# The last matrix product of a two-block transformer in fp32: 24 of its 32 row tiles by seven block products instead of eight, in two parts

## The chip, the core and the metric

One Trainium2 chip, one core. The time is device microseconds (us) of one launch of the whole kernel. An engine named PE is the matrix unit (TensorE), PEld its weight loads, DVE the vector engine, ACT the scalar engine, POOL the GpSimd engine, SP the sync engine, which here only starts transfers.

## What is computed

The input is x of 512 rows by 1024 columns, everything in fp32. Block one has two layers, each an attention and a SwiGLU network with layer norms; block two is one layer of a gated mixer and a network with a squared ReLU. Only the end of block two matters here:

```python
f = rmsnorm(h, pre_ff_g[l]) @ w_ff1[l]            # (512 x 1024) @ (1024 x 4096)
f = jnp.square(jax.nn.relu(f)) @ w_ff2[l]         # (512 x 4096) @ (4096 x 1024)
h = h + rmsnorm(f, post_ff_g[l])
```

The change concerns the product with `w_ff2`, called f2 below.

## The kernel before

**Precision.** Every fp32 operand v is split into hi (v rounded to the matrix unit's fp32r type) and lo = v - hi, and each product is three passes, hi*hi, hi*lo and lo*hi, accumulated in PSUM. For weights, ACT writes hi (line 125) and DVE subtracts to get lo (line 128); both land in a pair of 128 x 1024 tiles.

**Weights.** The class `Weights` streams all weights of the kernel in one list. A *spec* is one load of up to 512 KB into a raw tile (SP queue, line 79); a *unit* is what is split into one hi/lo pair. There are three raw buffers (`wraw`, line 244) and five pairs (line 245). When the matmuls of a unit are issued, `done` (line 157) frees it and `fill` (line 147) issues the splits of the unit five places ahead and the loads for which a raw buffer is free. SP takes its transfers strictly in the order written; a load waits there until the earlier readers of its buffer are through.

**Products by seven.** Some of the earlier products (`FAST`, `FAST1`, line 45) already go by Winograd's seven block products: two 2 x 2 block matrices are multiplied with seven products of blocks instead of eight, at the price of sums of blocks before and after. There the blocks of the weights are made on DVE (lines 100 to 107), the results are joined by the class `Blocks` (line 461). For these a raw buffer can be lent from another pool (`lent`, `lender`, lines 68 and 1308). `in_tiles` (line 429) runs the product with `w_ff1` (f1); its results, after ReLU and square, stand transposed in the tiles `h2` and `h3` (lines 1287 to 1317): 32 tiles of 128 x 512, tile k holding rows k of the inner 4096 for all 512 tokens.

**The last product, f2.** `Out` (line 364) and `out_phase` (line 387), called on line 1349. For each of the 32 row tiles k of `w_ff2`: load 512 KB, split it (ACT and DVE), split `h` tile k (lines 769 and 770, into `sh` and `sl`), then for each of four token tiles t three passes over two column halves, 24 matmuls of 128 x 128 by 128 x 512 on line 381. All eight PSUM banks are in use: four token tiles by two halves. The first 28 row tiles go k by k over all four t; the last four go t by t, so that the closing norm of one t (`finish_ff`, line 1322, and `last_tile`, line 1326) runs beside the matmuls of the next. This tail is not changed.

Order on the engines: the instructions are put in order by a scheduler from the program's order and their dependencies; SP alone keeps the written order (line 249).

Of the kernel before, what the change touches and what calls it, by code (L numbers as in the profile page):

```python
# [10 lines left out]
F32 = mybir.dt.float32  # L11
# [32 lines left out]

FAST, FAST1 = range(4, 22), range(4, 14)
# [9 lines left out]
class Weights:  # L55


    def __init__(self, nc, raw, pairs, specs, units, lent, n_raw, n_pairs):
        self.nc, self.raw, self.pairs, self.specs, self.units, self.lent = nc, raw, pairs, specs, units, lent
        self.room, self.n_pairs, self.lender = [n_raw, 1], n_pairs, None  # L60
        self.loaded, self.split, self.released = 0, 0, 0
        self.r, self.p, self.extra = {}, {}, set()

    def load(self, parts=0):
        i = self.loaded
        src, (a, b), n = self.specs[i]

        t = self.lender() if i in self.lent else self.raw.tile([128, 1024], F32, name="wraw")
        v = t[:, :a * b].rearrange("p (a b) -> p a b", a=a)
        if n is not None:  # L70
            self.nc.gpsimd.memset(t[:, :a * b], 0.0)
            v = v[:, :, :n]
        self.r[i] = t
        self.loaded += 1
        self.room[i in self.lent] -= 1
        if parts:
            part = lambda a, m: a[:, m * a.shape[1] // parts:(m + 1) * a.shape[1] // parts]
            return lambda m: self.nc.sync.dma_start(part(v, m), part(src, m))
        self.nc.sync.dma_start(v, src)

    def _used(self, i):
        self.room[i in self.lent] += 1
        return self.r.pop(i)

    def _source(self, i, part):
# [4 lines left out]
        while self.loaded <= i + (part not in (None, 0)):  # L90
            self.load()
        if part is None:
            return self._used(i)[:, :], None
# [7 lines left out]
        tt = self.nc.vector.tensor_tensor  # L101
# [9 lines left out]
    def _split(self, pool, steps=1, name=None):  # L111
# [10 lines left out]
        def step(steps):  # L122
            for s in steps:
                sl = slice(s * n, (s + 1) * n)
                self.nc.scalar.activation(hi[:, sl], t[:, sl], AF.Copy)  # L125
                if between:
                    between()
                self.nc.vector.tensor_tensor(lo[:, sl], t[:, sl], hi[:, sl].bitcast(F32), op=OP.subtract)  # L128
# [7 lines left out]
    def _loads(self):  # L136
        while self.loaded < len(self.specs) and self.room[self.loaded in self.lent]:
            self.load()
# [27 lines left out]
def body(ctx, tc, ins, out, stop=None, dbg=None):  # L166
# [11 lines left out]
    specs, units, lent, at = [], [], set(), {}  # L178

    def spec(key, w, r0, nk, c0, n, pad=None, unit=True):  # L180
# [3 lines left out]
        specs.append((cols(w, r0, nk, c0, n), (nk, pad or n), n if pad else None))  # L184

    def spec_pair(key, w, c0, c1, fast):
# [5 lines left out]
        for m, c in ((1, c1), (0, c0)) if fast else ((0, c0), (1, c1)):  # L192
            if fast and key[-1] >= 7 and len(specs) % 4 == 0:
                lent.add(len(specs))
# [45 lines left out]
    rows("f2", ins["w_ff2_2"], 32)  # L240
# [16 lines left out]
    W = Weights(nc, raw, pairs, specs, units, lent, 3, 5)  # L257

# [105 lines left out]
    class Out:  # L364


        def __init__(self, key, order, operand):
            self.key, self.order, self.operand = key, list(order), operand
            self.banks, self.act = {}, {}

        def __call__(self, k, t, halves=(0, 1)):
# [7 lines left out]
            for n, (a, b) in enumerate(((0, 0), (0, 1), (1, 0))):  # L379
                for c in halves:  # L380
                    nc.tensor.matmul(self.banks[t][c], act[a][:, ts(t)], w[b][:, 0, c * 512:(c + 1) * 512],  # L381
                                     start=first and n == 0, stop=last and n == 2)
# [4 lines left out]
    def out_phase(o, finish, after, tail, spare=None, last=None):  # L387
# [3 lines left out]
        head = o.order[:-tail]  # L391
# [6 lines left out]
        for t in range(NT):  # L398
# [8 lines left out]
            finish(t, o.banks[t])  # L407

# [372 lines left out]
    def ffn(l, tails, finish, after):  # L781
        with tc.tile_pool(name="h", bufs=6) as hp:
            four = [hp.tile([128, 4 * S], F32, name="h4") for _ in range(6)]
            h = [t[:, n * S:n * S + S] for t in four for n in range(4)]
            with tc.tile_pool(name="blocks", bufs=1) as bp:
# [5 lines left out]
                W.lender = lambda: room  # L791
# [511 lines left out]
    with tc.tile_pool(name="blocks2", bufs=1) as bp:  # L1303
# [9 lines left out]
        W.lender = lender  # L1313
# [3 lines left out]
    parts[1] = es3.enter_context(tc.tile_pool(name="h3", bufs=1)).tile([128, 4, S], F32, name="h3")  # L1317
    in_tiles(f1(14, 16), lambda n, p: evac_f1(n + 28, p))
    hs = es3.enter_context(tc.tile_pool(name="hs2", bufs=5))
# [6 lines left out]
    def last_tile(o, ks):  # L1326
# [47 lines left out]
```

## Time and profile before

| what | us |
|---|---|
| median of three runs (1737.64 to 1738.59) | 1737.68 |
| the profiled execution, own time | 1737.9 |
| its span, first to last instruction | 1736.2 |
| PE busy in the span | 1716.8 (99%) |
| DVE busy | 1202.5 (69%) |
| ACT busy | 858.2 (49%) |
| granted clock of PE over the span | 0.999 of full speed |

The profile is of one execution. Busy is the sum of an engine's instructions over the span of 1736.2 us. Matmuls overlap one another, so a busy share of PE near 100% says that it always had work, not how fast one matmul follows another; for that a run of matmuls is divided by its count. The time of the execution is 1.7 us more than its span.

### The profile page before, as it was taken

The numbers are of one execution on the slowest core, as the hardware profiler recorded it, in microseconds if no ns is written. First come the engines' busy times: TensorE is split into PE (matmuls) and PEld (weight loads), VectorE is DVE, ScalarE is ACT, GpSimd is POOL, SyncE is SP. The second block draws the span as 40 slices with busy tenths as digits, with TensorE's granted clock in tenths as the row PEclk, the third lists the DMA queues.
The fourth block names the chain that finished last, engine by engine and source line by source line (L and its number), as shares of the span: only waits on it lengthen the run. The fifth ranks groups of instructions, "written<-read, shape, count | busy, mean of one in ns | idle before, by whom it ended". The sixth has DMA issues, their size and how long they took to land.

```text
span 1736.2 us, 27322 instructions
## 1 busy us (share of the span) xinstructions
PE 1716.8 (99%) x10748; PEld 1531.6 (88%) x10748; DVE 1202.5 (69%) x2034; ACT 858.2 (49%) x1437; POOL 128.6 (7%) x237
## 2 busy tenths in 40 slices
PE   8999999999999999999999999999999999999998
PEld 8888889999978888888899999888877899988886
DVE  6888866999944656666789998346646588953333
ACT  6877633444533367777444445333525345652221
POOL 0312102000000012220000000001001100000000
PEclk9999999999999999999999999999999999999999
DMA  6544345434344245552333334331422223343331
GB/s 205 136 100 110 98 141 165 132 99 122 109 136 121 76 118 129 133 137 77 97 98 108 112 100 156 109 99 50 125 69 89 82 80 110 110 134 97 98 97 50
DMA packets 207202, 191.60 MB, mean 110 GB/s; under 512 B 8800, under 2 KB 176928, under 8 KB 207072
## 3 DMA queue, kind: packets, MB, share of 16 engines
q1 hardware_dynamic: 194384, 162.48, 31.8%
q0 software_dynamic: 12112, 25.52, 6.6%
q8 instruction: 85, 1.39, 0.3%
q10 hardware_dynamic: 576, 1.84, 0.3%
q14 instruction: 45, 0.37, 0.1%
HBM read 172.99 MB, written 7.38 MB: 104 GB/s over the span
## 4 chain that ended last, share of the span: by engine, by line
PE 91%; DVE 4%; ACT 3%; issue 1%; DMA 1%; POOL 0%; ACTq 0%; SPq 0%; POOLq 0%; DVEq 0%
PE ps L295 54%; PE ps L381 30%; PE ps L908 1%; PE ps L896 1%; PE ps L311 1%; PE ps L589 1%; PE ps L590 1%; DVE wlo L128 1%; ACT whi L125 1%; ACT x L634 1%; PE ps L695 0%; PE ps L719 0%; PE ps L1108 0%; PE ps L1113 0%; DMA x<-in_x 0%
## 5 line engine op out<-in xcount | busy, mean ns | idle before, releaser
L125 ACT ACTIVATE whi<-wraw 128x1024 fp32r<-128x1024 f32 (+2 forms) x332 | 332.9, 1010 | 290.8 <-PE ps L295 146.5
L128 DVE TENSOR_TENSOR wlo<-wraw,whi 128x1024 fp32r<-128x1024 f32 (+2 forms) x332 | 385.0, 1163 | 124.5 <-ACT whi L125 121.6
L295 PE MATMUL ps<-xh,whi 128*128 128x256 f32 (+1 forms) x1232 | 387.1, 316 | 1.0 <-ACT xh L313 1.0
L295 PE MATMUL ps<-xl,whi 128*128 128x256 f32 (+1 forms) x1232 | 385.4, 313 | 0.5 <-DVE xl L314 0.3
L295 PE MATMUL ps<-xh,wlo 128*128 128x256 f32 (+1 forms) x1232 | 385.6, 313 | 0.0
L295 PEld LDWEIGHTS ps<-xh,whi 128*128 128x128 f32 x1232 | 233.6, 190 | 14.4 <-ACT xh L313 2.4
L295 PEld LDWEIGHTS ps<-xh,wlo 128*128 128x128 f32 x1232 | 234.5, 190 | 12.9
L295 PEld LDWEIGHTS ps<-xl,whi 128*128 128x128 f32 x1232 | 234.6, 190 | 12.4 <-DVE xl L314 1.0
L295 PE MATMUL ps<-th,whi 128*128 128x256 f32 x736 | 204.2, 277 | 0.0
L295 PE MATMUL ps<-tl,whi 128*128 128x256 f32 x736 | 203.8, 277 | 0.0
L295 PE MATMUL ps<-th,wlo 128*128 128x256 f32 x736 | 203.5, 276 | 0.0
L295 PEld LDWEIGHTS ps<-tl,whi 128*128 128x128 f32 x736 | 138.5, 188 | 0.1
L295 PEld LDWEIGHTS ps<-th,whi 128*128 128x128 f32 x736 | 138.5, 188 | 0.1
L295 PEld LDWEIGHTS ps<-th,wlo 128*128 128x128 f32 x736 | 138.3, 188 | 0.0
L295 PE MATMUL ps<-whi,xh 128*128 128x256 f32 (+1 forms) x384 | 124.5, 324 | 0.0
L295 PE MATMUL ps<-whi,xl 128*128 128x256 f32 (+1 forms) x384 | 122.6, 319 | 0.0
L295 PE MATMUL ps<-wlo,xh 128*128 128x256 f32 (+1 forms) x384 | 122.5, 319 | 0.0
L381 PE MATMUL ps<-whi,th 128*128 128x512 f32 x312 | 96.8, 391 | 1.3 <-DVE h L523 1.1
L381 PE MATMUL ps<-whi,tl 128*128 128x512 f32 x312 | 96.1, 389 | 0.0
L381 PE MATMUL ps<-wlo,th 128*128 128x512 f32 x312 | 96.1, 389 | 0.0
L290 POOL TENSOR_TENSOR ln_st<-rs_in,mhalf 128x1 f32<-128x1 f32 x39 | 27.5, 704 | 824.6 <-DVE rs_in L289 817.6
L770 DVE TENSOR_TENSOR tl<-h,th 128x512 fp32r<-128x512 f32 x44 | 29.8, 690 | 79.1 <-ACT th L769 79.0
(347 smaller groups left out, 3139.2 us busy)
## 6 DMA issues: line engine op xcount, KB each, us to landing
wraw<-in_ffn_w_in SPq DMA_DIRECT2D x73, 512.0 KB, 4.8
wraw<-in_w_ff SPq DMA_DIRECT2D x60, 512.0 KB, 4.1
wraw<-in_ffn_w_out SPq DMA_DIRECT2D x44, 512.0 KB, 3.7
wraw<-in_a_w_qkv SPq DMA_DIRECT2D x23, 512.0 KB, 5.1
wraw<-in_w_in SPq DMA_DIRECT2D x20, 512.0 KB, 3.7
wraw<-in_kv_w SPq DMA_DIRECT2D x16, 512.0 KB, 3.9
room<-in_ffn_w_in SPq DMA_DIRECT2D x15, 512.0 KB, 3.9
copies<-extd POOLq DMA_DIRECT2D x16, 320.0 KB, 8.5
```

Source lines behind the costliest of these rows:

```text
L125: self.nc.scalar.activation(hi[:, sl], t[:, sl], AF.Copy)
L128: self.nc.vector.tensor_tensor(lo[:, sl], t[:, sl], hi[:, sl].bitcast(F32), op=OP.subtract)
L290: nc.gpsimd.tensor_tensor(r, u[:, :n], mhalf[:, :n], op=OP.pow)
L295: nc.tensor.matmul(ps, lhs[a][lsel], rhs[b][rsel], start=first and n == 0, stop=last and n == 2)
L311: nc.tensor.transpose(p[:, k, :], y[:, ts(4 * c + k)], ident)
L381: nc.tensor.matmul(self.banks[t][c], act[a][:, ts(t)], w[b][:, 0, c * 512:(c + 1) * 512], start=first and n == 0, stop=last and n == 2)
L589: yield lambda: nc.tensor.matmul(p[:, :N], part[m][:, ts(i)], part[2 + m][:, :N], start=True, stop=False)
L590: yield lambda: nc.tensor.matmul(p[:, :N], part[m][:, ts(i)], part[4 + m][:, :N], start=False, stop=True)
L634: nc.scalar.activation(qs[32 * g:32 * g + 32], p[32 * (g ^ 1):32 * (g ^ 1) + 32], AF.Copy)
L770: nc.vector.tensor_tensor(lo, src[k], hi.bitcast(F32), op=OP.subtract)
L896: nc.tensor.transpose(p[:, j], e[:, ts(j)], ident)
L908: nc.tensor.matmul(p[:, q0:], v, aT[q][:, kt, q0:], start=kt == 0 and q == 0, stop=kt == NT - 1 and q == 1)
```

## The change

Twenty-four of the 32 row tiles of f2 are taken as twelve pairs q (`TWO = 12`). Of a pair, the activations form a 2 x 2 block matrix (two token halves of 256 by two row tiles of 128) and the weights another (two row tiles by two column halves of 512). The seven products are run in two parts, because their sums don't all fit in PSUM at once:

- **Part A**, for q = 0 to 11: four products, S1, S2, A11 and S3, each summed over all q into two of the eight banks. One product is six matmuls of 128 x 128 by 128 x 512 (two token tiles, three passes). Weights: two units per pair, both 1024 columns wide, made from one full row tile (512 KB) and one half row tile (256 KB) by three DVE sums (part "a0").
- **Between**: the banks are combined in place, with ACT copies and DVE sums in PSUM, so that they hold what the remaining products add to.
- **Part B**, for q = 0 to 11: three products, A12, S4 and A22, added to six of the banks that now hold the combined sums (A12 and S4 to the banks of token tiles 0 and 1, A22 to two of tiles 2 and 3). Weights: both row tiles are loaded again (2 x 512 KB); one unit is a whole raw tile ("b0"), the other 512 columns made by three DVE sums ("b1"). After q = 2 and q = 5 two ordinary row tiles (24, 25 and 26, 27) run in the old way. Row tiles 28 to 31 remain the tail.

The blocks of the activations are made per two pairs, by `first` for part A (four DVE sums, four splits) and by `then` for part B (three splits). Their hi and lo parts for the later pairs go to the tiles `xh` and `xl`, free once f1 is done.

For 30 of the 48 weight units of the pairs, lo is made without DVE: ACT writes -hi, and a transfer on POOL's queue adds the raw tile to it (`accum_op`), 512 KB each. In part A these are the first unit of each pair and the second unit of the odd pairs (18), in part B the first unit of each pair (12). Three more raw buffers are lent to f2 (two `y` tiles and half of `gb`), one load of each pair going to them (from q = 2 on in part A).

The diff, cut to its core (empty lines are left out):

```diff
--- before.py
+++ after.py
@@ -42,6 +42,9 @@
 TAIL, SPARE = (6, 7), ((11, 12), (10, 11, 12, 14))
+TWO, LENT2 = 12, {"a": (0, 1, 0, 1), "b": (0, 1, 0, 1)}
 FAST, FAST1 = range(4, 22), range(4, 14)
@@ -57,29 +60,30 @@
     def __init__(self, nc, raw, pairs, specs, units, lent, n_raw, n_pairs):
         self.nc, self.raw, self.pairs, self.specs, self.units, self.lent = nc, raw, pairs, specs, units, lent
-        self.room, self.n_pairs, self.lender = [n_raw, 1], n_pairs, None
+        self.room, self.n_pairs, self.lender = [n_raw, 1, 3], n_pairs, [None, None]
         self.loaded, self.split, self.released = 0, 0, 0
-        self.r, self.p, self.extra = {}, {}, set()
+        self.r, self.p, self.extra, self.added = {}, {}, set(), set()
     def load(self, parts=0):
...
-        t = self.lender() if i in self.lent else self.raw.tile([128, 1024], F32, name="wraw")
-        v = t[:, :a * b].rearrange("p (a b) -> p a b", a=a)
+        src, (a, b), n, c = self.specs[i]
+        place = self.lent.get(i, 0)
+        t = self.lender[place - 1]() if place else self.raw.tile([128, 1024], F32, name="wraw")
+        v = t[:, c:c + a * b].rearrange("p (a b) -> p a b", a=a)
...
-        self.room[i in self.lent] -= 1
+        self.room[place] -= 1
...
     def _used(self, i):
-        self.room[i in self.lent] += 1
+        self.room[self.lent.get(i, 0)] += 1
         return self.r.pop(i)
     def _source(self, i, part):
@@ -87,8 +91,28 @@
-        while self.loaded <= i + (part not in (None, 0)):
+        while self.loaded <= i + (part not in (None, 0, "b0")):
             self.load()
+        tt = self.nc.vector.tensor_tensor
+        if part in ("a0", "b1"):
+            (e0, e1), (o0, o1) = ((t[:, :512], t[:, 512:]) for t in (self.r[i + (part == "b1")], self.r[i + (part == "a0")]))
+        if part == "a0":
+            tt(o0, e1, e0, op=OP.subtract)
+            tt(e1, o1, e1, op=OP.subtract)
+            tt(o1, o1, o0, op=OP.subtract)
+            return self._used(i + 1)[:, :], None
+        if part == "a1":
+            return self._used(i)[:, :], None
+        if part == "b0":
+            return self.r[i][:, :], None
+        if part == "b1":
+            tt(e1, e1, e0, op=OP.subtract)
+            tt(e1, e1, o1, op=OP.subtract)
+            tt(e0, o0, e1, op=OP.add)
+            self._used(i)
+            return self._used(i + 1)[:, :512], None
         if part is None:
             return self._used(i)[:, :], None
         if part == 0:
@@ -98,7 +122,6 @@
         if part == 3:
             return self._used(i + 1)[:, :], None
         (a11, a12), (a21, a22) = ((t[:, :512], t[:, 512:]) for t in (self.r[i + 1], self.r[i]))
-        tt = self.nc.vector.tensor_tensor
         tt(a22, a21, a22, op=OP.add)
         tt(a21, a11, a21, op=OP.subtract)
@@ -125,6 +148,11 @@
                 self.nc.scalar.activation(hi[:, sl], t[:, sl], AF.Copy)
                 if between:
                     between()
+                if self.split in self.added:
+                    self.nc.scalar.activation(lo[:, sl], t[:, sl], AF.Copy, scale=-1.0)
+                    self.nc.gpsimd.dma_start(lo[:, sl], t[:, sl], accum_op=OP.add)
+                    continue
                 self.nc.vector.tensor_tensor(lo[:, sl], t[:, sl], hi[:, sl].bitcast(F32), op=OP.subtract)
         step(range((steps + 1) // 2))
...
+    w, added = ins["w_ff2_2"], set()
+    def spec_two(key, q, kind, transfer):
+        for n in range(2):
+            at[key, kind, q, n] = len(units)
+            if n in transfer:
+                added.add(len(units))
+            units.append((len(specs), kind + str(n)))
+        for odd in (0, 1) if kind == "a" else (1, 0):
+            c = 512 if kind == "a" and odd else 0
+            if LENT2[kind][(2 * q + odd) % 4] and (kind == "b" or q > 1):
+                lent[len(specs)] = 2
+            specs.append((cols(w, 256 * q + 128 * odd, 1, c, 1024 - c), (1, 1024 - c), None, c))
+    for q in range(TWO):
+        spec_two("f2", q, "a", (0, 1) if q % 2 else (0,))
+    second = []
+    for q in range(TWO):
+        second.append(("b", q))
+        spec_two("f2", q, "b", (0,))
+        if q % 3 == 2 and 2 * TWO + 2 * (q // 3) + 2 <= 28:
+            for k in range(2 * TWO + 2 * (q // 3), 2 * TWO + 2 * (q // 3) + 2):
+                second.append(("one", k))
+                spec(("f2", k), w, 128 * k, 1, 0, D)
+    tail_f2 = [k for k in range(2 * TWO, 32) if ("one", k) not in second]
+    for k in tail_f2:
+        spec(("f2", k), w, 128 * k, 1, 0, D)
...
@@ -366,7 +423,7 @@
         def __init__(self, key, order, operand):
             self.key, self.order, self.operand = key, list(order), operand
-            self.banks, self.act = {}, {}
+            self.banks, self.act, self.ran = {}, {}, set()
         def __call__(self, k, t, halves=(0, 1)):
             if t not in self.banks:
@@ -379,7 +436,8 @@
             for n, (a, b) in enumerate(((0, 0), (0, 1), (1, 0))):
                 for c in halves:
                     nc.tensor.matmul(self.banks[t][c], act[a][:, ts(t)], w[b][:, 0, c * 512:(c + 1) * 512],
-                                     start=first and n == 0, stop=last and n == 2)
+                                     start=first and n == 0, stop=last and n == 2,
+                                     skip_group_check=self.order[0] < 0)
         def done(self, k):
             W.done(at[self.key, k])
@@ -388,7 +446,7 @@
-        head = o.order[:-tail]
+        head = [k for k in o.order[:-tail] if k >= 0 and k not in o.ran]
         for n, k in enumerate(head):
             if spare and n in spare[0]:
                 spare[1]()
@@ -405,6 +463,92 @@
                 if t >= 2 and n == tail // 2 - 1:
                     after(t - 2)
             finish(t, o.banks[t])
+    def two_parts(o, key, n_two, second, view, slots, tmp, z5):
+        tt, order = nc.vector.tensor_tensor, [-1, *o.order]
+        for t in range(NT):
+            o.banks[t] = [bank(), bank()]
+        o.order = order
+        parts = {}
+        def split(b, name, v):
+            hi, lo = slots(b, name)
+            nc.scalar.activation(hi, v, AF.Copy)
+            tt(lo, v, hi.bitcast(F32), op=OP.subtract)
+            parts[b, name] = hi, lo
+        def blocks(b):
+            v = view(b)
+            return [v[:, :, tile, half] for half in range(2) for tile in range(2)]
+        def first(b):
+            (a11, a12, a21, a22), (s1, s2) = blocks(b), tmp
+            tt(s1, a21, a22, op=OP.add)
+            split(b, "S1", s1)
+            tt(s2, s1, a11, op=OP.subtract)
+            split(b, "S2", s2)
+            split(b, "A11", a11)
+            tt(a21, a11, a21, op=OP.subtract)
+            split(b, "S3", a21)
+            tt(a11, a12, s2, op=OP.subtract)
+        def then(b):
+            a11, a12, a21, a22 = blocks(b)
+            split(b, "A12", a12)
+            split(b, "S4", a11)
+            split(b, "A22", a22)
+        def product(unit, half, q, name, t0, c, begin):
+            w, act = W.get(at[unit]), parts[q // 2, name]
+            for m in range(2):
+                for n, (i, j) in enumerate(((0, 0), (0, 1), (1, 0))):
+                    nc.tensor.matmul(o.banks[t0 + m][c], act[i][:, q % 2, ts(m)], w[j][:, 4 * half:4 * half + 4],
+                                     start=begin and n == 0, stop=False, skip_group_check=True)
+        u = [t.rearrange("p a b -> p (a b)") for t in tmp]
+        def part_a():
+            first(0)
+            for q in range(n_two):
+                if q % 2 == 0 and q + 2 < n_two:
+                    first(q // 2 + 1)
+                product((key, "a", q, 0), 0, q, "S1", 0, 1, q == 0)
+                product((key, "a", q, 0), 1, q, "S2", 2, 1, q == 0)
+                W.done(at[key, "a", q, 0])
+                product((key, "a", q, 1), 0, q, "A11", 0, 0, q == 0)
+                if q == n_two - 1:
+                    then(0)
+                    for m in range(2):
+                        nc.scalar.activation(z5[:, m], o.banks[m][1], AF.Copy)
+                        nc.scalar.activation(u[m], o.banks[m][0], AF.Copy)
+                        tt(u[m], o.banks[2 + m][1], u[m], op=OP.add)
+                product((key, "a", q, 1), 1, q, "S3", 2, 0, q == 0)
+                W.done(at[key, "a", q, 1])
+        part_a()
+        for m in range(2):
+            tt(o.banks[m][1], o.banks[m][1], u[m], op=OP.add)
+        for m in range(2):
+            tt(o.banks[2 + m][0], o.banks[2 + m][0], u[m], op=OP.add)
+            tt(o.banks[2 + m][1], o.banks[2 + m][0], z5[:, m], op=OP.add)
+        for kind, q in second:
+            if kind == "one":
+                for t in range(NT):
+                    o(q, t)
+                o.done(q)
+                continue
+            if q % 2 == 0 and q + 2 < n_two:
+                then(q // 2 + 1)
+            product((key, "b", q, 0), 0, q, "A12", 0, 0, False)
+            product((key, "b", q, 0), 1, q, "S4", 0, 1, False)
+            W.done(at[key, "b", q, 0])
+            product((key, "b", q, 1), 0, q, "A22", 2, 0, False)
+            W.done(at[key, "b", q, 1])
     def out_units(o):
         ks = [(t, k) for t in range(2) for k in range(5)] + [(t, k) for k in (5, 6) for t in range(2)]
...
@@ -1310,13 +1454,23 @@
                 room.append(yp.tile([128, D], F32, name="y"))
             return room[0]
-        W.lender = lender
+        lend2 = []
+        def lender_f2():
+            n = len(lend2)
+            lend2.append(yp.tile([128, D], F32, name="y") if n < 2 else gb[:, 1] if n == 2 else lend2[n - 3])
+            return lend2[n]
+        W.lender = [lender, lender_f2]
         blocks = Blocks([h[:, 14:18], h[:, 18:22]], th, tl, lambda: yp.tile([128, D], F32, name="y"))
         in_tiles(f1(0, 14), evac_f1, 5,
                  [[], [lambda: after_mix(2)], [], [], [lambda: after_mix(3)]], fast_f1, side_steps(blocks.steps(), 0, 2))
-    parts[1] = es3.enter_context(tc.tile_pool(name="h3", bufs=1)).tile([128, 4, S], F32, name="h3")
+    hp3 = es3.enter_context(tc.tile_pool(name="h3", bufs=1))
+    parts[1] = hp3.tile([128, 4, S], F32, name="h3")
     in_tiles(f1(14, 16), lambda n, p: evac_f1(n + 28, p))
-    hs = es3.enter_context(tc.tile_pool(name="hs2", bufs=5))
+    hs = es3.enter_context(tc.tile_pool(name="hs2", bufs=4))
+    tmp, z5 = (hp3.tile([128, 2, 512], F32, name=n) for n in ("sums", "z5"))
     nc.sync.dma_start(gb[:, 0], bcast(ins["post_ff_g_2"], D))
     def finish_ff(t, banks):
@@ -1346,8 +1500,22 @@
         for k in ks:
             o.done(k)
-    out_phase(Out("f2", range(32), splitter(lambda k: [hs.tile([128, S], F32R, name="s" + n) for n in "hl"], [at_h(k)[:, 0] for k in range(32)])), finish_ff, lambda t: None, 4,
-              last=last_tile)
+    o = Out("f2", [*(k for kind, k in second if kind == "one"), *tail_f2],
+            splitter(lambda k: [hs.tile([128, S], F32R, name="s" + n) for n in "hl"], [at_h(k)[:, 0] for k in range(32)]))
+    halves = lambda t: t.rearrange("p (q s) -> p q s", q=2)
+    turn = []
+    def slots(b, name):
+        if b == 0 and name in ("A11", "S1", "S2", "S3"):
+            return [halves(hs.tile([128, S], F32R, name="s" + n)) for n in "hl"]
+        turn.append(name)
+        return [halves(t[:, len(turn) % 8]) for t in (xh, xl)]
+    two_parts(o, "f2", TWO, second, lambda b: h[:, 4 * b:4 * b + 4].rearrange("p (q e) (f s) -> p q e f s", q=2, f=2), slots,
+              [halves(tmp[:, n]) for n in range(2)], z5)
+    o.ran.update(k for kind, k in second if kind == "one")
+    out_phase(o, finish_ff, lambda t: None, 4, last=last_tile)
 _INS = ["x", "a_w_qkv", "a_lambda", "a_subln_g", "a_w_o", "kv_w", "b_w_q", "b_rel_bias", "b_w_o", "ln_g", "ln_b",
```

## Rows read from the trace of the kernel before

**Rows 1.** The page's first part: busy time, share of the span, instructions.

```profile
PE 1716.8 (99%) x10748; PEld 1531.6 (88%) x10748; DVE 1202.5 (69%) x2034; ACT 858.2 (49%) x1437; POOL 128.6 (7%) x237
```

**Rows 2.** The chain that ended last, 1380 to 1740: start, us, what, count.

```profile
1404.79 150.56 PE ps L295 x1128
1555.36 157.55 PE ps L381 x695
```

**Rows 3.** Windows: end of f1, and f2; busy us, clock, DMA share, GB/s.

```profile
1532.00:1555.00 23.00, 23.00 (x110) 19.27 (x109) 12.98 (x17) 10.36 (x15) 0.00 (x0) 1.00 0.43 135
1555.00:1700.00 145.00, 145.00 (x641) 120.09 (x640) 51.72 (x54) 42.74 (x54) 0.00 (x0) 1.00 0.32 95
```

**Rows 4.** Groups by line and shape, 1555 to 1705: busy us, mean ns, idle before.

```profile
L381 PE MATMUL ps<-whi,sh 128*128 128x512 f32 x221 | 68.0, 389 | 0.0
L128 DVE TENSOR_TENSOR wlo<-wraw,whi 128x1024 fp32r<-128x1024 f32 x28 | 34.3, 1226 | 10.6 <-ACT whi L125 10.6
L125 ACT ACTIVATE whi<-wraw 128x1024 fp32r<-128x1024 f32 x28 | 29.3, 1046 | 3.9 <-PE ps L295 3.9
L770 DVE TENSOR_TENSOR sl<-h,sh 128x512 fp32r<-128x512 f32 x27 | 18.7, 693 | 87.8 <-ACT sh L769 87.8
L769 ACT ACTIVATE sh<-h 128x512 fp32r<-128x512 f32 x27 | 17.1, 635 | 103.9 <-PE ps L381 103.9
```

**Rows 5.** Timeline of DVE and ACT, 1526 to 1567: start, us, engine, line, what.

```profile
1533.82 0.68 DVE L770 TENSOR_TENSOR sl<-h,sh 128x512 fp32r<-128x512 f32 x1
1534.41 0.69 DVE L522 TENSOR_TENSOR gb<-ps,y 128x512 f32<-128x512 f32 x1
1535.94 1.22 DVE L128 TENSOR_TENSOR wlo<-wraw,whi 128x1024 fp32r<-128x1024 f32 x1
1537.08 0.69 DVE L526 TENSOR_TENSOR y<-ps,gb 128x512 f32<-128x512 f32 x1
...
1527.97 1.06 ACT L125 ACTIVATE whi<-wraw 128x1024 fp32r<-128x1024 f32 x1
1528.93 1.05 ACT L1300 ACTIVATE h<-h 128x1024 f32<-128x1024 f32 x1
...
1560.38 0.64 ACT L769 ACTIVATE sh<-h 128x512 fp32r<-128x512 f32 x1 [3.67 <-PE ps L381]
1560.92 1.05 ACT L125 ACTIVATE whi<-wraw 128x1024 fp32r<-128x1024 f32 x1
```

**Rows 6.** DMA queues and issues, 1555 to 1710: packets, MB, share; us to landing.

```profile
q1 hardware_dynamic: 3763, 13.68, 29.3%
...
wraw<-in_w_ff SPq DMA_DIRECT2D x25, 512.0 KB, 3.5
```

**Rows 7.** The same of the whole span: POOL's queue, its issues, KB, us to landing.

```profile
q0 software_dynamic: 12112, 25.52, 6.6%
...
copies<-extd POOLq DMA_DIRECT2D x16, 320.0 KB, 8.5
bias<-copies POOLq DMA_DIRECT2D x16, 256.0 KB, 3.1
...
kl<-gb POOLq DMA_DIRECT2D x28, 128.0 KB, 5.2
```

**Rows 8.** Timeline of POOL, four transfers issued one after the other.

```profile
52.41 2.05 POOL L577 DMA_DIRECT2D kl<-gb  x4
```

**Rows 9.** Windows near the start, same columns as rows 3.

```profile
5.00:10.00 5.00, 3.77 (x15) 2.79 (x15) 3.17 (x6) 3.46 (x8) 0.00 (x0) 1.00 1.07 330
10.00:15.00 5.00, 5.00 (x37) 5.00 (x36) 2.38 (x5) 2.06 (x4) 0.00 (x0) 1.00 1.05 374
```

**Rows 10.** Waits of SP's queue, 1440 to 1710: us in total, times, longest.

```profile
SPq L79 <- DVE wlo L128: 232.9, 50, 9.7
```

More of the change, by code (lines that the diff above doesn't have):

```diff
@@ L59, in __init__ @@
         self.nc, self.raw, self.pairs, self.specs, self.units, self.lent = nc, raw, pairs, specs, units, lent
-        self.room, self.n_pairs, self.lender = [n_raw, 1], n_pairs, None
+        self.room, self.n_pairs, self.lender = [n_raw, 1, 3], n_pairs, [None, None]
         self.loaded, self.split, self.released = 0, 0, 0
-        self.r, self.p, self.extra = {}, {}, set()
+        self.r, self.p, self.extra, self.added = {}, {}, set(), set()
     def load(self, parts=0):
         i = self.loaded
-        src, (a, b), n = self.specs[i]
-        t = self.lender() if i in self.lent else self.raw.tile([128, 1024], F32, name="wraw")
-        v = t[:, :a * b].rearrange("p (a b) -> p a b", a=a)
+        src, (a, b), n, c = self.specs[i]
+        place = self.lent.get(i, 0)
+        t = self.lender[place - 1]() if place else self.raw.tile([128, 1024], F32, name="wraw")
+        v = t[:, c:c + a * b].rearrange("p (a b) -> p a b", a=a)
         if n is not None:
@@ L136, in _loads @@
     def _loads(self):
-        while self.loaded < len(self.specs) and self.room[self.loaded in self.lent]:
+        while self.loaded < len(self.specs) and self.room[self.lent.get(self.loaded, 0)]:
             self.load()
@@ L175, in cols @@
         return bass.AP(tensor=w.tensor, offset=w.offset + r0 * ld + c0, ap=[[ld, 128], [128 * ld, nk], [1, n]])
-    specs, units, lent, at = [], [], set(), {}
+    specs, units, lent, at = [], [], {}, {}
     def spec(key, w, r0, nk, c0, n, pad=None, unit=True):
@@ L183, in spec @@
             units.append((len(specs), None))
-        specs.append((cols(w, r0, nk, c0, n), (nk, pad or n), n if pad else None))
+        specs.append((cols(w, r0, nk, c0, n), (nk, pad or n), n if pad else None, 0))
     def spec_pair(key, w, c0, c1, fast):
@@ L193, in spec_pair @@
             if fast and key[-1] >= 7 and len(specs) % 4 == 0:
-                lent.add(len(specs))
+                lent[len(specs)] = 1
             spec((key, "one", m), w, 0, 8, c, 128, unit=not fast)
@@ L239, in body @@
         spec_pair(("f1", f), ins["w_ff1_2"], 256 * f, 256 * f + 128, f in FAST1)
-    rows("f2", ins["w_ff2_2"], 32)
+    w, added = ins["w_ff2_2"], set()
[23 more added lines that the diff above has]
+        spec(("f2", k), w, 128 * k, 1, 0, D)
     const = ctx.enter_context(tc.tile_pool(name="const", bufs=1))
@@ L257, in body @@
     W = Weights(nc, raw, pairs, specs, units, lent, 3, 5)
+    W.added = added
     def load_x(t):
@@ L790, in ffn @@
                 room = bp.tile([128, 2 * S], F32, name="room")
-                W.lender = lambda: room
+                W.lender[0] = lambda: room
                 def evac(n, p):
```

## The prediction

> **What bounds the kernel now.** I read the page's busy shares first: PE has work 99% of the span, DVE 69%, ACT 49%, POOL 7% [rows 1]. The chain of waits says whether that work sets the end: from 1404.79 to 1712.9 it is nothing but PE, 1128 matmuls of line 295 (f1) and then 695 of line 381 (f2) [rows 2]. The 695 took 157.55 us, so one matmul follows another every 0.2267 us, though its own row says 389 ns [rows 2, 4]; matmuls overlap, and the pace is the price. Over f2 the windows show PE at 145.00 of 145.00 us at the full granted clock, its 2.4 GHz level, with DVE busy 51.7, ACT 42.7, POOL 0 and the transfers at a share of 0.32 [rows 3]. So the last product is bound by the number of its matmuls, everything else in it has room, and a matmul less is worth 0.2267 us as long as everything else keeps up..
>
> **What goes.** A pair of row tiles was 2 x 24 = 48 matmuls; seven products of six are 42. Twelve pairs: 72 fewer, of the same shape (512 columns), 72 x 0.2267 = **16.3 us**. Of the 768, 696 stay: part A 12 x 24 = 288 (65.3 us), part B 12 x 18 + 4 x 24 = 312 (70.7 us), the tail 96. The products keep one bank for three matmuls and change the loaded weights each time; the 512-column matmuls of line 295 just before f2 do that too, and the chain shows no gap there, so I take the same pace.
>
> **DVE and ACT.** From the starts of back-to-back instructions, a DVE sum of 512 columns holds the engine 0.60 us (1533.82 to 1534.41) and one of 1024 columns 1.14 (1535.94 to 1537.08); an ACT copy takes 0.54 (1560.38 to 1560.92) and 0.96 (1527.97 to 1528.93) [rows 5]. Part A, per pair, beside 24 x 0.2267 = 5.44 us of PE:
> - DVE: three sums of weights 1.8; one lo of 1024 for every second pair 0.57; of `first`, per two pairs four sums and four lo, 2.4 per pair. Sum 4.8.
> - ACT: two hi 1.92; -hi for 1.5 units 1.44; half of four splits 1.08. Sum 4.4.
>
> Part B, beside 18 x 0.2267 = 4.08 us: DVE 1.8 + 0.6 + 0.9 = 3.3; ACT 1.92 + 0.54 + 0.81 = 3.3. Both engines stay under PE, at 88% and 82% in A, 81% and 80% in B. With full durations (0.69 and 1.22) [rows 4, 5] DVE in part A would be 5.4, just PE's time; so it could stand level with PE but not far over it. The cover is five pairs split ahead. I charge 1 us for part A.
>
> **Start.** `first(0)` needs eight DVE instructions (4.8 us) and four of ACT before the first product; its data, the first four tiles of h, were done long before. In the last 23 us of f1 DVE is busy 13.0 and ACT 10.4 [rows 3], of which five splits of h go. It fits: 0.
>
> **Between the parts.** After A11 of the last pair come S3 and A12 (1.36 us each), then S4, which waits for two ACT copies out of PSUM, two DVE sums into u, and the sum into its bank; A22 waits for two more. At 0.60 each (a DVE sum out of PSUM is no dearer: 0.69 long, line 522 [rows 5]) S4's bank is ready some 2.8 us after A11 ends, when S4 is due at 2.7; A22's at 4.0 to 4.6, due at 4.1. The lo of three splits of `then(0)`, 1.8 us, may stand ahead of them. 0 to 2.5 us; I take 1.
>
> **Transfers.** Before, f2 read one 512 KB tile per row tile: 13.68 MB moved in 155 us at a share of 29.3%, that is 301 GB/s while busy, 1.74 us of all sixteen DMA engines per tile, landing 3.5 us after issue [rows 6]. Now part A loads 9.4 MB, part B 14.7, 24.1 together, 80 us at that rate. To it come 30 accumulating transfers of 512 KB. The trace has none, so I bound one. From below: as a load, 1.74. POOL's own queue, nearest in kind since it moves data within the core too, made 25.52 MB in 6.6% of 1736 us, 223 GB/s: 2.35 each [rows 7]. From above: twice that, 4.7, if the bytes it adds to must be fetched as well. The sums over both parts, against 136.0 us of PE, are 80 + 52 = 132, 80 + 71 = 151 and 80 + 141 = 221. But busy shares aren't capacity: near the start the engines moved 330 and 374 GB/s at shares just over 1 [rows 9]; by 374 all 39.9 MB take 107 us, and some 2 MB of part A's loads lie ahead of it. I take a price between 1.74 and 2.35, at which the transfers just fit; what they then cost is latency.
>
> **Latency.** A unit's pair comes free five units ahead; four units' time remains: 10.9 us in part A, 8.2 in B (two pairs). A unit by transfer needs two ACT copies, 2.0 us with a wait, POOL's issue, 0.5 (four took 2.05 [rows 8]), and the landing: 3.5 for a load of that size [rows 6], 3.1, 5.2 and 8.5 for rows on POOL's queue [rows 7]. 6 to 11 us in all. Part A hides that. In part B the period of a pair can't be under half of it: at a landing of 6, among full queues, 4.25 to 4.4 us instead of 4.08, over ten or so pairs 2 to 3 us; at 8.5, 5.5 us, 12 to 17. The raw buffers say the same: SP already waits for the last reader of each, 232.9 us in 50 waits [rows 10], and that reader is now the transfer: three buffers, each 3.5 to load, 2.5 to copy and issue and 6 to land, 12 us against 3 x 4.08 = 12.2. The four ordinary row tiles give back some. I take 4 us. SP issues 56 loads instead of 32, at 0.33 each; it is idle otherwise. Behind a transfer on POOL wait only later transfers; its other work starts in the tail. The tail itself is the same: 0.
>
> **Sum.** The profiled execution took 1737.9 us (span 1736.2 and 1.7 around it): 1737.9 - 16.3 + 1 + 1 + 4 = 1727.6. The median of the runs lies 0.2 lower; so **1727.4 us**.
>
> **Rivals.**
> *The transfers bind: slower.* One mechanism: an accumulating transfer fetches what it adds to, so 30 of them are 31.5 MB and not 15.7, and the DMA engines, not PE, set the pace of both parts. Then 24.1 + 31.5 = 55.6 MB take 149 us at 374 GB/s [rows 9] and 185 at 301 [rows 6]: 13 to 49 us over PE's 136. The middle, 31, gives 1721.4 + 31 = 1752. It is slower than before once a transfer holds all sixteen engines for more than (136.0 + 16.3 - 80) / 30 = 2.4 us, which is next to the 2.35 of POOL's queue. For it: that closeness, and shares that already reach 1 when loads crowd. Against it: the unused 0.68 of the share in f2 [rows 3], and rates over 301 when crowded. The Trainium skill, DMA: Bandwidth & Descriptors, Rules for kernel authors, says that an accumulate reads its destination and writes it later; by that rule the fetch is real and this rival's bytes are the right ones. The same page, Issuing engines are not separate DMA queues, has transfers of SP and POOL run on the same sixteen engines, so that POOL's come out of the loads' share. No row here shows either.
>
> *Latency eats the gain: no change.* Landings like the 8.5 us row [rows 7] hold part B at 5.5 us per pair: 17 us less what the ordinary tiles hide, with 1 + 1 from above about 1735 to 1740. For it: only five pairs and three raw buffers. Against it: the 8.5 us row issues eight transfers at once.
>
> *DVE in step with PE.* At full durations part A loses up to 0.5 us a pair, 6 in all: 1727 to 1733, still faster; it is inside my forecast's own range.
>
> **How the numbers follow.** About 0.2% (3.5 us) is what a measurement of this kernel can tell from no change: faster means under 1734.2, slower over 1741.2. Forecast 0.58; latency 0.14; transfers bind 0.25; other mishaps on the slow side 0.03. The forecast's own range is 1721 (only the matmuls count) to 1733 (DVE level with PE, a landing of 7 us). For 8 in 10 I add the latency case to 1741 and half of the transfers' case, to its middle, 1752. Faster 0.58; same 0.15 (latency, with the low end of the transfers' case); slower 0.27.
>
> **What would show it.** Right: 10676 matmuls on the page; PE gapless in part A with the chain on it, DVE near 88% there; a gap of about a us at the change of parts; gaps in part B of a few tenths per pair, which end on a transfer into `wlo`, landing 5 to 7 us after issue; a transfer share around 0.9. Transfers binding: landings that grow along part A beyond 9 us, a share of 1 throughout, PE idle in both parts until `wlo` by transfer or until `wraw`, POOL waiting for nothing. Latency: PE idle in part B only, the share well under 1, landings about 8 us from the first on. DVE: PE waiting for `wlo` of line 128 or for the splits of `first`, DVE without gaps. The forecast is wrong if PE loses more than 10 us in the two parts together, or if the pace of matmuls within a product isn't 0.227.

## The result and the profile after

| | us |
|---|---|
| before, median of the runs beside it | 1738.13 |
| changed kernel, median of four (1750.13 to 1752.50) | 1751.12 |
| ratio, with its 95% interval | 1.0078 (1.0066 to 1.0091) |
| forecast, and its range | 1727.4 (1721 to 1752) |

The change makes the kernel slower by 13 us. The time lies just inside the range, on the wrong side of no change, and within 1 us of the middle of the first rival, 1752. In the changed kernel line 510 is the matmul of the block products, 438 that of `Out`, 148 and 156 write hi and lo of a weight, 153 writes -hi, 154 is the accumulating transfer, 83 the load, 102 to 104 and 111 to 113 the sums of weights.

The page's first part says that the 72 matmuls are gone and PE is idle more, 98% for 99% [rows 1]:

```profile
PE 1711.9 (98%) x10676; PEld 1522.8 (87%) x10676; DVE 1262.7 (72%) x2150; ACT 916.6 (52%) x1513; POOL 154.9 (9%) x267
```

The first matmul of part A in PE's timeline (start, length), and windows, columns as in [rows 3]: from 1555.20, where f2 began in the kernel before, to the first matmul of S4; from there to the tail (306 matmuls, 69.4 us at the old pace); and the turn between the parts by itself:

```profile
1553.95 0.39 PE L510 MATMUL ps<-whi,sh 128*128 128x512 f32 x1
```

```profile
1555.20:1646.70 91.50, 73.69 (x291) 57.53 (x289) 58.71 (x91) 57.23 (x75) 15.67 (x18) 0.90 0.93 227
1646.70:1719.50 72.80, 72.80 (x307) 59.74 (x308) 44.05 (x65) 37.85 (x48) 7.85 (x9) 0.96 0.90 249
...
1640.00:1653.00 13.00, 9.24 (x21) 6.79 (x22) 10.88 (x18) 5.50 (x9) 0.87 (x1) 0.50 0.72 179
```

Part A and A12 are 294 matmuls, 66.6 us at the old pace. From 1553.95 to 1646.69 they took 92.7, 26.1 us too many; the first window starts five or six of them late. The second stretch has 3.4 too many. In the first PE has nothing running for 17.8 us (91.50 - 73.69): 10.5 inside part A, and 7.3 in two gaps at the turn, which are shown further down. The other 8 go to slower matmuls, for the granted clock is 0.90 on the mean. DVE and ACT are busy 64% and 63% there, so neither is full. The DMA engines are, at a share of 0.93, yet they move only 227 GB/s. In the second stretch PE has no gap.

What PE waited for in the first stretch (waits: us in total, times, longest; the gap of 3.4 us before S4 ends just behind it), and below it SP's queue:

```profile
PE ps L510 <- DMA wlo<-wraw: 9.1, 4, 3.2
PE ps L510 <- ACT sums L528: 3.9, 1, 3.9
PE ps L510 <- DMA wlo<-y: 0.8, 1, 0.8
```

```profile
SPq L83 <- DMA wlo<-wraw: 34.3, 6, 8.6
SPq L83 <- DVE wlo L156: 28.7, 6, 6.3
```

The DMA queues and issues of 1555 to 1646.5, columns as in [rows 6]:

```profile
q0 software_dynamic: 2594, 9.45, 55.8%
q1 hardware_dynamic: 3744, 11.27, 37.3%
...
wraw<-in_w_ff SPq DMA_DIRECT2D x14, 512.0 KB, 6.2
wlo<-y POOLq DMA_DIRECT2D x9, 512.0 KB, 6.6
wlo<-wraw POOLq DMA_DIRECT2D x5, 512.0 KB, 9.3
```

q0 is POOL's queue, here nothing but the accumulating transfers: 55.8% of 91.5 us for 9.45 MB, which is 18 of 0.524 MB, so **2.83 us of all sixteen engines each**, where the forecast took 1.74 to 2.35. Loads land after 6.2 us, 3.5 before [rows 6]. Eighteen transfers (51 us) and 9.4 MB of loads at q1's rate here (11.27 MB in 34.1 us: 28.5 us) are 80 us of work for engines that had 65. Part A took 86 (1553.95 to 1640.36).

The chain of waits near the end of part A (start, us, what) touches PE for 3.2 us only and runs from transfer to load to transfer:

```profile
1597.30 7.94 DMA wlo<-wraw
...
1606.04 4.64 DMA gb<-in_w_ff
...
1611.87 9.31 DMA wlo<-wraw
...
1621.22 3.24 PE ps L510 x9
1624.46 8.15 DMA gb<-in_w_ff
```

### The profile page after: what moved, and what is told of

Same layout as the page of the kernel before. It is cut to its first block, busy times and chain, and to the rows that moved or that the text cites. A ratio compares the mean times of both kernels' runs of the same rounds, so it can differ in the third digit from the quotient of the medians.

```text
span 1749.0 us, 27568 instructions
## 1 busy us (share of the span) xinstructions
PE 1711.9 (98%) x10676; PEld 1522.8 (87%) x10676; DVE 1262.7 (72%) x2150; ACT 916.6 (52%) x1513; POOL 154.9 (9%) x267
## 4 chain that ended last, share of the span: by engine, by line
PE 86%; DMA 4%; DVE 4%; ACT 3%; issue 2%; POOL 0%; SPq 0%; DVEq 0%; POOLq 0%; ACTq 0%
PE ps L352 53%; PE ps L438 23%; PE ps L510 3%; DMA wraw<-in_w_ff 1%; DMA wlo<-wraw 1%; DMA gb<-in_w_ff 1%; PE ps L1052 1%; PE ps L1040 1%; PE ps L368 1%; PE ps L733 1%; PE ps L734 1%; ACT x L778 1%; ACT whi L148 1%; DVE wlo L156 1%; PE ps L839 0%
## 5 line engine op out<-in xcount | busy, mean ns | idle before, releaser
L156 DVE TENSOR_TENSOR wlo<-wraw,whi 128x1024 fp32r<-128x1024 f32 (+2 forms) x326 | 371.1, 1141 | 111.2 <-ACT whi L148 108.2
L913 ACT ACTIVATE th<-h 128x512 fp32r<-128x512 f32 x44 | 26.9, 628 | 99.1 <-PE ps L438 74.8
```

The source lines that it names most:

```text
L913: nc.scalar.activation(hi, src[k], AF.Copy)
```

## The experiments

Three theories stood at the start. Theory 1: raw buffers are held until their transfers have landed. Theory 2: the sixteen engines are full. Theory 3: sums that wait for a load block the queues of DVE and ACT. Edits are against the changed kernel.

**Without transfers** (e1).

```diff
-    W.added = added
+    W.added = set()
```

> All lo parts go back to DVE (the set of units by transfer is empty); the result is the same. In the changed kernel part A took 91.5 us (1555.2 to 1646.7) where its 288 matmuls need 65.3, and part B 72.8 where they need 70.7. Theory 1 (buffers): a raw buffer is held until the transfer that reads it has landed, so the loop load, sums, copies, transfer, next load sets part A. Theory 2 (engines full): the sixteen DMA engines can't move more. Theory 3 (order): sums that wait for a load block DVE and ACT for what stands behind them. Without transfers, theories 1 and 2 both expect loads that land in about 4 us and a part A set by DVE: 12 pairs x (4.8 + 1.5 x 1.14) = 78 us, part B 73 to 76, 1737 to 1741 us in all. Theory 3 expects part A no shorter than 88, since DVE's queue is fuller than before.

Measured: 1729.68 us, ratio to before 0.9953 (0.9933 to 0.9972). That is 21 us less than with the 30 transfers, and 7 less than before. Its window, which runs 4.6 us past S4's start (1626.61), and its loads:

```profile
1555.20:1631.20 76.00, 72.38 (x312) 57.74 (x310) 75.44 (x105) 43.12 (x61) 0.00 (x0) 1.00 0.46 146
```

```profile
wraw<-in_w_ff SPq DMA_DIRECT2D x13, 512.0 KB, 3.7
```

DVE is busy 75.4 of 76.0 us, as expected, and PE waits only for lo of DVE and hi of ACT; loads land in 3.7. The expected total was 8 us too high because of part A: it took not 78 us but 68.5 (first product at 1556.73, A12 at 1625.22), 3.2 over its matmuls, for PE lived on its lead and was busy 44.8 of 44.8 us to 1600. From A12 to the tail it took 75.0, within the 73 to 76 expected. Theory 3 is out as the main cause: DVE's queue was fuller, part A far shorter. So the transfers cost more than the DVE time they save. Which property of them does, the next three tell.

**Fewer transfers** (e2).

```diff
-        spec_two("f2", q, "a", (0, 1) if q % 2 else (0,))
+        spec_two("f2", q, "a", (0,))
```

> Transfers only for the first unit of each pair: 12 in part A instead of 18, none of them from the buffers that the full row tiles use; part B as it is. The result is the same. DVE in part A: 12 x (4.8 + 0.57) = 64 us, just under PE. Theory 1 (buffers): those buffers are free again after DVE's lo; part A 66 to 72 us, 1725 to 1732 in all. Theory 2 (engines full): transfers were 0.56 of the share of 0.93, a third of them goes, so part A 91.5 x (0.37 + 0.37) / 0.93 = 73 to 76, 1733 to 1737. Theory 3 (order): 85 or more, 1745 or more.

Measured: 1740.25 us, ratio 1.0020 (1.0007 to 1.0032); eight runs between 1736.0 and 1745.1. The same stretch took 81.1 us at a share of 0.88:

```profile
1555.20:1636.30 81.10, 69.18 (x288) 55.09 (x286) 63.79 (x96) 51.89 (x70) 11.15 (x13) 0.96 0.88 220
```

The full row tiles were no longer held by a transfer, yet loads still landed in 5.9. Theory 1's 1725 to 1732 is missed by 8 us; theory 2 (73 to 76, 1733 to 1737) is nearer, and still too low.

**Plain copies** (e3).

```diff
-                    self.nc.gpsimd.dma_start(lo[:, sl], t[:, sl], accum_op=OP.add)
+                    self.nc.gpsimd.dma_start(lo[:, sl], t[:, sl])
```

> The 30 transfers copy the raw tile over lo instead of adding to it: the same bytes written, nothing fetched from the destination, the same waits. This changes the computation: lo is wrong in those units. If the fetch is what makes a transfer dear (2.85 us of all engines over f2), the share per transfer falls to about 1.9 and they land in about 5 us instead of 7.4; theory 2 (engines full) then expects part A at 75 to 80 us, theory 1 (buffers) at 75 to 82, since the hold gets 2 to 3 us shorter. If the fetch costs nothing, both expect 90 to 92.

Measured (one execution): 1730.84 us, 20 less than the changed kernel with as many transfers, bytes written and waits. Window, queue and issues to 1628:

```profile
1555.20:1628.30 73.10, 66.65 (x292) 54.25 (x290) 57.84 (x90) 57.61 (x76) 9.53 (x18) 1.00 0.85 278
```

```profile
q0 software_dynamic: 2528, 9.24, 34.9%
...
wlo<-y POOLq DMA_DIRECT2D x9, 512.0 KB, 4.4
wlo<-wraw POOLq DMA_DIRECT2D x5, 512.0 KB, 6.8
```

A plain copy holds the engines for 34.9% of 73 us over 17.6 transfers, 1.45 us: half of 2.83. The price and the 73.1 us of the stretch are both below what was expected (1.9 and 75). The copies land 2.2 and 2.5 us sooner, and the engines move 278 GB/s. Adding in flight, not transferring, is what costs. This run doesn't separate the engines' time from the landings, which fell with it.

**Another source** (e4).

```diff
-                    self.nc.gpsimd.dma_start(lo[:, sl], t[:, sl], accum_op=OP.add)
+                    self.nc.gpsimd.dma_start(lo[:, sl], self.fixed[:, sl], accum_op=OP.add)
...
-    W.added = added
+    W.added, W.fixed = added, x[0]
```

> The 30 transfers add a tile that nobody writes (the first token tile of the residual) instead of the raw tile: the same bytes, the same engines, the same waits for ACT before them, but the raw buffer is free when ACT and DVE have read it. This changes the computation: lo is wrong in those units. Theory 1 (buffers): part A falls to 66 to 74 us, 1725 to 1733 in all. Theory 2 (engines full): part A stays at 88 to 92. Theory 3 (order): between, 80 or more, since loads land as late as before.

Measured (one execution): 1746.40 us, 4.7 less. SP's waits for a buffer now end on DVE and ACT, none on a transfer, and the stretch was 86.8 us at nearly the same price, 2.73 us each:

```profile
1555.20:1642.00 86.80, 70.17 (x290) 55.57 (x289) 57.72 (x90) 57.13 (x75) 15.63 (x18) 0.95 0.91 224
```

```profile
q0 software_dynamic: 2624, 9.57, 57.3%
...
wlo<-x POOLq DMA_DIRECT2D x18, 512.0 KB, 7.7
```

So theory 1 is worth about 5 of the 21 us; the rest stays with the full engines and what lands late by them. Counted from each run's own first product to the first matmul of S4, the stretch is 92.7 us in the changed kernel, 69.9 in e1, 82.8 in e2, 73.9 in e3 and 88.1 in e4.

**Transfers that nobody needs** (e7). All lo parts on DVE, and beside them transfers into a scratch tile, up to pair 9.

```diff
-                    self.nc.scalar.activation(lo[:, sl], t[:, sl], AF.Copy, scale=-1.0)
-                    self.nc.gpsimd.dma_start(lo[:, sl], t[:, sl], accum_op=OP.add)
-                    continue
+                    if self.scratch is not None:
+                        self.nc.gpsimd.dma_start(self.scratch[:, sl], hi[:, sl].bitcast(F32), accum_op=OP.add)
```

> All lo parts on DVE as in the kernel that took 1729.7 us, and beside them accumulating transfers of 512 KB for the same units of part A up to pair 9 (those split after the scratch tile exists, 12 or 13), from hi into a scratch tile. PE, ACT and DVE wait for none of them but the last. The scratch is the tile z5, cleared on DVE. So the engines are loaded as in the changed kernel's part A, but nothing is late because a lo part lands late. If the crowd on the engines makes the loads late (theory 2 by way of the loads), loads land in 5.5 to 7 us instead of 3.7 and the time goes to 1738 to 1748. If what hurt was only that the lo parts themselves landed late, loads may land later but the time stays at 1729 to 1733.

Measured (one execution): 1741.71 us. It doesn't tell what it was made for. The transfers share one scratch tile, so each waited for the one before, and each held the hi tile it read:

```profile
POOL z L154 <- DMA z<-whi: 42.1, 8, 6.9
ACT whi L148 <- DMA z<-whi: 17.0, 6, 5.5
```

```profile
q0 software_dynamic: 1737, 6.33, 45.1%
...
z<-whi POOLq DMA_DIRECT2D x12, 512.0 KB, 5.2
wraw<-in_w_ff SPq DMA_DIRECT2D x9, 512.0 KB, 4.0
```

It does give the price and the landing of such transfers one at a time. These rows are of 1555 to 1630: 45.1% of 75 us over 12.1 transfers is 2.80 us of all engines each, and they land in 5.2. So the 2.83 of the changed kernel isn't made by several being in flight; with six transfers (e5, below) it is 2.90. One at a time they leave the loads at 4.0, where the changed kernel has 6.2. How much of the loss came through late loads and how much through late lo parts stays open.

**A few transfers** (e5, e6, e11). Six, in part A; the same with four in part B; twelve, in part B only.

```diff
-        spec_two("f2", q, "a", (0, 1) if q % 2 else (0,))
+        spec_two("f2", q, "a", (0,) if q % 2 else ())      # e5, e6; e11: ()
...
-        spec_two("f2", q, "b", (0,))
+        spec_two("f2", q, "b", ())      # e5; e6: (0,) if q % 3 == 0 else (); e11 as it was
```

> Transfers only for the first unit of the odd pairs of part A: 6 of the 30; all other lo parts on DVE. The result is the same. Theory 1 is down to a small part after the run with another source (1746.4 us); theory 2 stands as: an accumulating transfer holds all engines for 2.8 us (a plain copy 1.5), and 30 of them with the loads fill the engines, so that loads and transfers land late. Six need 17 us of the 60 that were free in part A without transfers (share 0.42). DVE in part A falls from 6.5 to 5.9 us per pair, 71 us. Theory 2 expects landings of loads near 4 us, 1725 to 1729 us in all, a little under the kernel without transfers (1729.7). If instead each transfer costs what it did among 30 (21 us more than without any, 0.7 each), 1733 to 1735.

> The same with four transfers in part B as well (first units of pairs 0, 3, 6, 9): 10 of the 30. The result is the same. DVE in part B falls from 4.4 to 4.1 us per pair, level with PE; the share there was 0.66 without transfers and becomes about 0.8. Theory 2 expects 1725 to 1729, within 2 us of the run with six. If any transfer in part B costs more than DVE's time that it saves, 1730 or more.

> Twelve pairs, the 12 transfers of part B as in the change, none in part A. The result is the same. In the changed kernel PE ran without a gap through part B with 12 transfers and a share of 0.90. If the harm is that part A holds 18 accumulating transfers in the 65 us that its matmuls need, while part B holds 12 in 71, this run takes what the one without any took, 1728 to 1731. If the transfers of part B hurt too (the first of them are made while part A ends), 1733 or more.

Measured: 1730.04 (ratio 0.9954, 0.9938 to 0.9971), 1732.49 (0.9963, 0.9950 to 0.9977) and 1733.92 (0.9987, 0.9977 to 0.9997). None beats the run without transfers, though with six the engines have room, loads land in 4.4 us and the transfers in 4.7. The first two miss theory 2's 1725 to 1729 by 1 and 3.5 us. The third falls to its other case, 1733 or more: the twelve of part B hurt too, by 4 us against e1 in the times and 6 in the ratios. The waits show where. With six (waits of PE, 1555 to 1700), and with twelve in part B (timeline of PE, where part B begins):

```profile
PE ps L510 <- DMA wlo<-y: 4.5, 3, 2.4
PE ps L510 <- DMA wlo<-gb: 0.6, 1, 0.6
```

```profile
1628.07 0.80 PE L510 MATMUL ps<-wlo,xh 128*128 128x512 f32 x1 [3.75 <-DMA wlo<-y]
```

In the kernel without transfers PE's waits on lo were 2.7 us in 3. I read it so: where DVE paces the stage, a unit's sums are ready only just in time, and a transfer puts its copy, issue and landing behind them. No run had the sums ready earlier to test that.

**Two sums on POOL** (e8), no transfers, from the second block on.

```diff
-            tt(a21, a11, a21, op=OP.subtract)
+            (tt if b == 0 else nc.gpsimd.tensor_tensor)(a21, a11, a21, op=OP.subtract)
...
-            tt(a11, a12, s2, op=OP.subtract)
+            (tt if b == 0 else nc.gpsimd.tensor_tensor)(a11, a12, s2, op=OP.subtract)
```

> No transfers, and from the second block on two of the four sums of activations in part A (S3, and the one for S4 that only part B needs) on POOL instead of DVE. The result is the same. The kernel without transfers (1729.7) is held by DVE: 99% busy in part A, 8 us over the 1721.4 that the matmuls alone would give. Five blocks x 2 x 0.60 = 6 us leave DVE. If DVE is the bound and POOL works beside it, 1724 to 1728. If POOL's sums hold up DVE (both read two operands) or come late, 1729 or more. No run has shown POOL's price for such a sum yet.

Measured: 1736.47 us, ratio 0.9998 (0.9988 to 1.0008); 7 us lost against e1, as its second case has it (1729 or more). Groups by line and shape, 1555 to 1640:

```profile
L496 POOL TENSOR_TENSOR h<-h 128x512 f32<-128x512 f32 x4 | 10.9, 2732 | 23.6 <-DVE sums L491 23.6
L498 POOL TENSOR_TENSOR h<-h,sums 128x512 f32<-128x512 f32 x5 | 9.5, 1891 | 20.2 <-DVE xl L482 14.6 <-ACT xh L481 5.6
```

```profile
L156 DVE TENSOR_TENSOR wlo<-wraw,whi 128x1024 fp32r<-128x1024 f32 x11 | 16.7, 1516 | 0.2 <-ACT whi L148 0.2
```

POOL takes 1.9 to 2.7 us for what DVE does in 0.60, and DVE's lo, 1226 ns before [rows 4] and 1218 in e1, takes 1516 on the mean beside it.

**Fewer pairs** (e9, e10, e12), no transfers; e12 has three, for the first units of pairs 0 to 2.

```diff
-TWO, LENT2 = 12, {"a": (0, 1, 0, 1), "b": (0, 1, 0, 1)}
+TWO, LENT2 = 8, {"a": (0, 1, 0, 1), "b": (0, 1, 0, 1)}      # e9; e10, e12: 10
```

> No transfers and only eight pairs by seven products; the other 16 row tiles in the old way. The result is the same. 48 matmuls fewer than before, 10.9 us: 1726.6 at best. With twelve pairs PE had no gap in the first eight pairs of part A (PE busy 44.8 of 44.8 us), since five units lay ready; if that lead is what carries DVE's excess of 1.06 us per pair, eight pairs lose 0 to 2 us: 1726 to 1729. If the loss lies in the change of parts, it stays: 3 to 5 us, 1730 to 1732.

> No transfers and ten pairs. The result is the same. 60 matmuls fewer than before, 13.6 us: 1723.9 at best. DVE's excess over ten pairs is 10.6 us against a lead of four units, 10.9: 1724 to 1728 if the lead carries it, 1729 to 1732 if the loss of the twelve pairs lies in the change of parts.

> Ten pairs, and transfers only for the first units of the first three pairs, which are split while five units lie ready; none later. The result is the same. This takes 3.4 us from DVE where part A begins. The ten pairs without transfers took 1728.1, 4.2 over what their matmuls give, about 2 of it in waits for DVE's lo in part A. If these transfers land behind the lead, 1725 to 1728; if they land too late even there, as most of the six did, 1728 to 1731.

Measured: 1728.60 (ratio 0.9956, 0.9941 to 0.9971), **1728.13** (0.9949, 0.9934 to 0.9963) and 1730.56 (0.9962, 0.9948 to 0.9977). From the first product to A12 the profiled executions lost 1.4 us with eight pairs and 1.1 with ten, against 3.2 with twelve (e1), so the lead of five units carries most of DVE's excess. Eight pairs came out in their range, ten just over theirs (1724 to 1728), with 3.6 us lost from S4 to the tail. In their times 8, 10 and 12 pairs can't be told apart by these runs. The three early transfers don't help. Ten pairs without transfers has the lowest median found: 9.3 us less than before, 23 less than the change.

## Why the prediction was wrong

- **What goes: right.** 10676 matmuls, 72 fewer, one every 0.227 us wherever PE ran at the full clock. 1721 stood as the floor.
- **Transfers: the step that failed.** I bounded an accumulating transfer by 1.74, 2.35 and 4.7 us of all sixteen engines and took "a price between 1.74 and 2.35, at which the transfers just fit", so my sum has nothing for engines that are full. It was 2.83 in the changed kernel, 2.80 one at a time (e7), and half of that, 1.45, as a plain copy. The price agrees with the Trainium skill, DMA: Bandwidth & Descriptors, Rules for kernel authors, as cited in the rival, that an accumulate reads its destination. With 2.83 the same sum over both parts is 80 + 85 = 165 us, 29 over PE's 136. POOL's average of 2.35, the row that I leaned on, was no near row: I read that queue as moving data within the core, but 37% of its bytes are `copies` and `bias` [rows 7], which go to or come from DRAM tiles (lines 818 to 847 of the kernel before), and it is dearer than a plain copy of this shape. The point at which I had the change turn slower was 2.4.
- **I added up both parts.** 136 us of PE against the sum of both hid that part A alone asks for 80 us of transfers in 65; its 18 transfers come every 3.6 us, part B's 12 every 5.9. PE lost 26 us up to S4 and had no gap from there on. That part B's twelve are not free either, the run with them alone shows (e11): 4 to 6 us, lost at the turn.
- **Latency: mis-placed.** I charged part B 4 us and part A nothing ("Part A hides that"). Part B's 3.4 us are no gaps but, for 3.2 of them, matmuls at half clock after the turn (last section). In part A two ACT copies (2.0), the issue (0.87) and a landing of 9.3 us pass the 10.9 of four units; with one of 6.6 they don't, and there the loads, at 6.2, came late as well.
- **Between the parts: 1 us taken, 0 to 2.5 given.** Two gaps, 3.87 and 3.40 us, in front of A12 and S4 (PE timeline; the idle time is in brackets):

```profile
1640.36 0.80 PE L510 MATMUL ps<-whi,xh 128*128 128x512 f32 x1 [3.87 <-ACT sums L528]
...
1646.69 0.80 PE L510 MATMUL ps<-whi,xh 128*128 128x512 f32 x1 [3.40 <-DVE ps L535]
```

  In ACT's timeline the copies into u stand behind a hi of part B that waited for its sums and their load, in DVE's the sums into u behind the same. Without transfers the wait for line 535 is gone from PE's list (e1); with plain copies it was still 4.5 us, and with two sums on POOL and no transfer 3.3 (e8). That speaks for theory 3 at this spot; another order here was not tried.
- **DVE and ACT: right.** With transfers DVE was under PE's time (58.7 us busy in the first stretch, against 12 x 4.8 = 57.6 worked out); without, 6.5 us per pair made it the bound. e1 lies about 8 us over the floor: 3.2 in part A, not the 13 that pacing from the start would cost, because of the lead, and 4.3 from S4 to the tail.
- **The rivals.** The transfers bind: the mechanism was right for part A, and a price of two plain copies fits its bytes. That it had the engines pace both parts was wrong, for from S4 on PE had no gap. Its time, 1752 for 1751.1, is partly luck: it is the middle of 13 to 49 us, and part of the loss is the turn and the clock, which it doesn't have. Its chance of 0.25 was too low, because I set a free share of 0.68 [rows 3] against a demand that I had not worked out stage by stage. Latency as the rival had it, with PE idle in part B only and the share well under 1, is refuted by the changed kernel's own windows. Late landings as a part of the loss are not: with the fetch gone the time falls 20 us, but the landings fall too (e3); with nothing but the buffers' hold gone it falls 5 (e4).

## What to carry to other kernels

Count a transfer's price in engine time before its landing, stage by stage: an accumulating one cost two plain ones here (2.83 and 1.45 us for 512 KB), and the stage with the least matmul time per transfer decides. When work is moved off an engine that is nearly full, first run it with the work left there; a few units of lead may pay much of the excess (9 of 13 us of part A here), and a transfer in its place puts its whole latency behind operands that come just in time. A sum moved to an idle engine may slow the one that it was meant to relieve.

## What the hardware showed that I had not expected

**The clock.** PE stood 3.9 us, worked 2.9, stood 3.4, and over 1640 to 1653 its granted clock was 0.50, the 1.2 GHz level. Matmuls followed each other every 0.43 us (1647.28, 1647.71) instead of 0.227, until 1652.8, after 6 us of work without a gap; then 1.00 again. That is 3.2 of the 3.4 us of the second stretch. Up to S4 the clock was 0.90, which turned 17.8 us of gaps into 26 us of loss. [Rows 3] show 1.00.

**POOL and DVE.** An accumulating transfer took POOL 0.87 us to issue (15.67 for 18), a plain one 0.53 (9.53 for 18, e3). The rise of DVE's lo from 1218 (e1) to 1516 ns beside POOL's sums agrees with the Trainium skill, SBUF — State Buffer, Who interferes with whom: a DVE instruction with two SBUF inputs contends with a GpSimd instruction that reads SBUF.

**Shares of the DMA engines.** At shares of 0.93, 0.90 and 0.85 they moved 227, 249 and 278 GB/s in the stretches above: a share near 1 tells that the engines are taken, not what they can carry.
